# Where the heads stage keeps its substitution matrix and its PSUM banks, and where the last MLP tiles are split: a two-layer attention and RWKV-7 trunk on one core

## The chip, the cores and the metric

One Trainium2 chip, of which the kernel uses one core. The metric is device time in microseconds of one execution. Three executions of the kernel before took 4080.47, 4091.8 and 4091.95 us (median 4091.8).

The core has five engines with a queue each, worked off in order: PE (TensorE, matmul), DVE (VectorE), ACT (ScalarE), POOL (GpSimd) and SP, which here only issues DMAs. SBUF is the working memory of 128 partitions, PSUM the eight banks (128 partitions of 512 f32 each) that PE writes its results to. A "span" is the time from the first to the last instruction of the one execution that was profiled.

## The reference, cut to what matters

Each of two layers normalises and modulates the tokens (1024 latent, 256 context), projects them once, and hands the columns to two groups of heads: eight heads of softmax attention and eight heads of an RWKV-7 recurrence that runs in both directions. Their outputs are joined, projected, and followed by a squared-ReLU MLP. The changed parts are the two groups of heads and the end of the last layer's MLP:

```python
def rwkv7_step(state, inp):                       # group B, per direction and head, over all tokens
    r, w, k, v, a, b = inp
    sa = jnp.einsum('dbhij,dbhj->dbhi', state, a)
    state = state * w[..., None, :] + sa[..., :, None] * b[..., None, :] + v[..., :, None] * k[..., None, :]
    return state, jnp.einsum('dbhij,dbhj->dbhi', state, r)

def attend(q, k, v):                              # group A
    s = jnp.einsum('bqhd,bkhd->bhqk', q, k).astype(jnp.float32) * MLA_SCALE
    p = jax.nn.softmax(s, axis=-1).astype(v.dtype)
    return jnp.einsum('bhqk,bkhd->bqhd', p, v)

def sq_relu_mlp(h, w1, w2):
    return jnp.square(jax.nn.relu(h @ w1)) @ w2

# ... per layer i
x = x + mx[2][:, None] * (jnp.concatenate([att_x, rw_x], axis=-1) @ w_out[i])
x = x + mx[5][:, None] * sq_relu_mlp(modulate(rmsnorm(x, norm2_g[i]), mx[3], mx[4]), w_mlp1[i], w_mlp2[i])
# ... after both layers
return rmsnorm(x, final_g)
```

## The kernel before

A layer runs in three stages: `phase_in` (projections), `heads` (both groups of heads), `phase_out` (output projection and MLP). Products that need full precision split each factor into a high part (an ACT cast to a shorter format) and a low part (the rest, a subtraction on DVE or POOL), and PE makes three matmuls of them.

**The planner.** A stage describes its work as units (`us(engine, ns, ...)`): an engine, an assumed duration, what it needs, what it writes, and for PE units the class of PSUM banks that the result goes to. `Units.run` plays these units through and so sets the order in which each engine's instructions stand; of the units that could start soonest it takes the one with the longest path behind it, shifted by a rank (`RANKS_HEADS` and others, added to the path of the units of that name). The durations, latencies and ranks are numbers in the code. At run time the engines follow that order and wait for each other by semaphores; the assumed durations no longer play a part.

**`heads`.** Two chains share the engines.

- The recurrence (`recurrence`) runs ten steps of 128 tokens in each direction. In a step PE makes the block matrices `A` ("blk", L377; DVE masks them, L381), ACT and DVE lay them out (`begin1`, L414; transpose into `AX`, L419), and then DVE solves 32 small triangular systems per partition by forward substitution: 31 rounds of `mult` (`tmp` = `AX` column times row of `Y`, L436) and `total` (`Y` += `tmp`, L440). `Y`, the matrix of the substitution, lies in SBUF; POOL sets it to unit rows beforehand (L422, L424). ACT copies it out (`end1`, L449), DVE transposes, PE makes products "m1" (L473) and "x2" (L485), and then the state goes through PE products z, u, s, y (L519, L528, L538, L549/L552) for each direction and half step, with ACT and DVE evictions (`S`, L542, L543).
- The attention (`attention`) takes each head and tile of 512 queries: PE tests all scores for their maximum ("max", L715; DVE reduces them, L717, L718), turns the maxima into a row ("rows", L723), makes the scores (L742; ACT takes the exponential into `P`, L747), sums `P` on POOL (`Ps`, L751, 128 columns at a time) and multiplies with the values (L736).

PSUM is divided into classes: three banks "g" for most products, two "x" for the maxima alone, two "z" for the state's products, one "o" for the values' sums. A unit waits for a free bank of its class.

**The last MLP tiles.** In the last layer most of the MLP's second product is made by `fast`; the last 512 hidden columns are left to `finish`, called for the 512-token tile a = 1, and for a = 2 in two parts of 256 tokens. Four tiles of `w2` are loaded into `R`. `finish` splits each of them when a pair of output rows needs it: for a = 1 by ACT (L967) and DVE (L969), for a = 2 once in each part by ACT and POOL (L969), 12 splits in all. It adds the products to `x` (L1558), and then `norm_units` makes the final norm: ACT squares (L877, L880), DVE sums them (`acc`, L881), PE sums over partitions (`qn`, L885), and DVE writes the output (L1570).

Of the kernel before, what the change touches and what calls it, by code (L numbers as in the profile page):

```python
# [99 lines left out]
def sp_ns(n, k=1):  # L100
# [6 lines left out]
RANKS_HEADS = {"mult": -23041, "m1": -18260, "total": 4579, "max": 115, "f3a": -11034, "scores": 327, "sums": 2772, "values": -13437, "y": -22140,  # L107
               "begin1": -12967, "rows": 691, "BKt": -29802, "f1": -1812, "put": -46488, "yp": -1704, "A": -4699, "f1a": -11490, "m1p": -12501,
               "halves": 9522, "end3": -17483, "f2": -881}
# [153 lines left out]
class Trunk:  # L263
# [36 lines left out]
    def heads(self, li, ard, bvd, pc, gated, ysd, kd, vd, qd, qrd, krr, catd):  # L300

        with ExitStack() as es:
            e1 = self.pool(es, "hd", 1)
            ps = self.pool(es, "hps", 1, space=PSUM)
            banks = {k: [ps.tile([128, 512], F32, name=f"ps_{k}{j}") for j in range(n)] for k, n in (("g", 3), ("x", 2), ("z", 2), ("o", 1))}
            tiles = {}


            for name, n, shape in (("YF", 1, [128, 32, 32]), ("AX", 1, [128, 32, 32]), ("XM", 1, [128, 32, 32]), ("Y", 1, [128, 32, 16]), ("tmp", 1, [128, 144]),
# [6 lines left out]
            us = Units(59, RANKS_HEADS, dict(PE=120, ACT=75, DVE=75, Pool=75, SP=2300), False, True, 0.745, 0.395, 100)  # L316
# [6 lines left out]
    def recurrence(self, us, tiles, li, ard, bvd, pc, gated, ysd, catd):  # L323
# [9 lines left out]
        YF, XT, XM, tmp, sq, rs8 = (tiles[k][0] for k in ("YF", "XT", "XM", "tmp", "sq", "rs8"))  # L333
# [3 lines left out]
        half = lambda e: slice(64 * e, 64 * e + 64)  # L337
        heads = [(p, e, half(e)) for p in range(4) for e in range(2)]
# [11 lines left out]
        def step(i):  # L350
            w = {}
# [19 lines left out]
            for d in range(2):  # L371
                for ph in range(2):
                    for e in range(2):
# [9 lines left out]
                        x = add(f"blk{d}", us("PE", 772, back(NA, "begin", "m1", "z0", "z1", "y0", "y1"), pe, 284, bank="g", r=[nar[d], nbv[d]], rows=61))  # L383
                        add("A", us("DVE:A", 707, [x], dve, free=x))


            for d in range(2):
                for ph in range(2):
# [7 lines left out]
                    x = add(f"tok{d}", us("PE", 470, [], pe, 213, bank="g", r=[nbv[d]], rows=121))  # L396
# [10 lines left out]
                x = add(f"tok{d}", us("PE", 480, [], pe, 213, bank="g", r=[nbv[d]], rows=121))  # L407
# [21 lines left out]
            b2 = us("DVE", 1261, w["begin"] + back(NX, "end3"), begin2)  # L429
            b2b = us("Pool", 907, back(NY, "end1"), begin2b)  # L430
# [50 lines left out]
            for d in range(2):  # L481
# [9 lines left out]
                x = add("x2", us("PE", 570, [m1a[d], e3b[0]], pe, bank="g", rows=15))  # L491
# [1236 lines left out]
```

## Time and profile before

| what | before |
|---|---|
| median of three runs | 4091.8 us (4080.47 to 4091.95) |
| the profiled execution | 4084.27 us |
| its span | 4082.5 us |
| PE busy | 3884.9 us (95%) |
| DVE busy | 2595.6 us (64%) |
| ACT busy | 1831.8 us (45%) |
| POOL busy | 1312.9 us (32%) |
| mean granted clock of PE | 0.956 |

On PE the heads stage lasts from 504 to 1166 us in the first layer and from 2615 to 3267 us in the second; `finish` begins at about 4011 us. [...]

### The profile page before, as it was taken

The numbers are of one execution on the slowest core, as the hardware profiler recorded it, in microseconds if no ns is written. First come the engines' busy times: TensorE is split into PE (matmuls) and PEld (weight loads), VectorE is DVE, ScalarE is ACT, GpSimd is POOL, SyncE is SP. The second block draws the span as 40 slices with busy tenths as digits, with TensorE's granted clock in tenths as the row PEclk, the third lists the DMA queues.
The fourth block names the chain that finished last, engine by engine and source line by source line (L and its number), as shares of the span: only waits on it lengthen the run. The fifth ranks groups of instructions, "written<-read, shape, count | busy, mean of one in ns | idle before, by whom it ended". The sixth has DMA issues, their size and how long they took to land.

```text
span 4082.5 us, 66855 instructions
## 1 busy us (share of the span) xinstructions
PE 3884.9 (95%) x26144; PEld 2982.8 (73%) x26144; DVE 2595.6 (64%) x4563; ACT 1831.8 (45%) x3113; POOL 1312.9 (32%) x1912
## 2 busy tenths in 40 slices
PE   6999999999999999999998999999999999999998
PEld 3766666766778888888887766766676678777777
DVE  4477277788747455555337477487877565767676
ACT  4355456676644122222115355556676643333333
POOL 1344254545631000000001244455544704333322
PEclk9999979999999999999999999878998999999999
DMA  6256622332342122222103144711232251111111
GB/s 212 73 171 197 222 81 86 97 91 64 92 159 87 58 78 88 78 73 82 37 32 134 58 160 154 237 47 52 81 103 75 69 201 37 52 47 42 52 55 49
DMA packets 279708, 394.21 MB, mean 97 GB/s; under 512 B 60512, under 2 KB 192576, under 8 KB 279392
## 3 DMA queue, kind: packets, MB, share of 16 engines
q1 hardware_dynamic: 278992, 389.36, 30.0%
q8 instruction: 205, 3.36, 0.3%
q14 instruction: 111, 0.91, 0.1%
q10 hardware_dynamic: 400, 0.59, 0.1%
HBM read 288.45 MB, written 101.42 MB: 95 GB/s over the span
## 4 chain that ended last, share of the span: by engine, by line
PE 71%; DVE 14%; ACT 3%; issue 3%; DMA 2%; POOL 1%; SPq 0%; DVEq 0%; POOLq 0%; ACTq 0%
PE qm L930 39%; PE pm_m L930 8%; PE ps_g L742 4%; DVE tmp L436 3%; PE ps_g L377 3%; DVE Y L440 3%; PE ps_o L736 2%; PE ps_x L715 2%; PE qm L943 1%; DVE nm L717 1%; DMA aw<-in_ada_w 1%; PE pm_n L1185 1%; PE ps_z L549 1%; PE ps_z L552 1%; PE ps_z L538 1%
## 5 line engine op out<-in xcount | busy, mean ns | idle before, releaser
L930 PE MATMUL qm<-hh,wh 128*128 128x512 f32 (+1 forms) x1488 | 556.1, 374 | 7.3 <-DVE x L1529 6.9
L930 PE MATMUL qm<-hh,wl 128*128 128x512 f32 (+1 forms) x1488 | 554.2, 372 | 0.7 <-DVE wl L969 0.7
L930 PE MATMUL qm<-hl,wh 128*128 128x512 f32 (+1 forms) x1488 | 554.3, 373 | 0.0
L751 POOL TENSOR_TENSOR Ps<-Ps,P 128x128 f32<-128x128 f32 x1024 | 442.3, 469 | 256.5 <-ACT P L747 255.5
L967 ACT CAST wh<-wr 128x1024 fp32r<-128x1024 f32 x149 | 155.7, 1045 | 440.8 <-PE qm L930 399.2
L930 PE MATMUL pm_m<-hh,wh 128*128 128x512 f32 (+4 forms) x896 | 339.8, 379 | 3.2 <-ACT o L1244 3.2
L930 PE MATMUL pm_m<-hl,wh 128*128 128x512 f32 (+4 forms) x896 | 330.4, 369 | 1.1 <-POOL hl L917 1.1
L930 PE MATMUL pm_m<-hh,wl 128*128 128x512 f32 (+4 forms) x896 | 331.1, 370 | 0.2 <-DVE wl L969 0.2
L930 PEld LDWEIGHTS qm<-hh,wh 128*128 128x128 f32 x1488 | 279.6, 188 | 65.7 <-DVE x L1529 9.0
L930 PEld LDWEIGHTS qm<-hh,wl 128*128 128x128 f32 x1488 | 279.8, 188 | 55.1 <-DVE wl L969 1.4
L930 PEld LDWEIGHTS qm<-hl,wh 128*128 128x128 f32 x1488 | 279.6, 188 | 55.2 <-DVE hl L1425 0.9
L1529 DVE SCALAR_TENSOR_TENSOR x<-qm,mods,x 128x512 f32<-128x512 f32 x280 | 196.5, 742 | 177.1 <-PE qm L930 176.8
L930 PE MATMUL qm<-uh,wl 128*128 128x512 f32 (+1 forms) x768 | 274.0, 357 | 2.1 <-DVE wl L969 2.1
L930 PE MATMUL qm<-uh,wh 128*128 128x512 f32 (+1 forms) x768 | 275.0, 358 | 0.0
L930 PE MATMUL qm<-ul,wh 128*128 128x512 f32 (+1 forms) x768 | 273.8, 357 | 0.0
L969 DVE TENSOR_TENSOR wl<-wr,wh 128x1024 fp32r<-128x1024 f32 x149 | 188.8, 1267 | 127.9 <-ACT wh L967 127.6
L717 DVE TENSOR_REDUCE nm<-ps_x 128x1 f32<-128x512 f32 (+1 forms) x400 | 222.5, 584 | 68.5 <-PE ps_x L715 66.6
L747 ACT ACTIVATE P<-ps_g 128x512 f32<-128x512 f32 (+1 forms) x336 | 192.2, 587 | 140.2 <-PE ps_g L742 118.8
L1452 DVE SCALAR_TENSOR_TENSOR x<-qm,mods,x 128x512 f32<-128x512 f32 x160 | 119.6, 749 | 196.0 <-PE qm L930 192.6
L436 DVE TENSOR_TENSOR tmp<-AX,Y 128x126 f32<-128x126 f32 (+22 forms) x620 | 224.3, 362 | 21.8 <-ACT AX L427 3.7
L440 DVE TENSOR_TENSOR Y<-Y,tmp 128x126 f32<-128x126 f32 (+22 forms) x620 | 212.7, 343 | 22.4
L930 PEld LDWEIGHTS pm_m<-hh,wh 128*128 128x128 f32 (+2 forms) x896 | 169.8, 190 | 67.1 <-issue 31.0
(348 smaller groups left out, 8786.3 us busy)
## 6 DMA issues: line engine op xcount, KB each, us to landing
wr<-in_w SPq DMA_DIRECT2D x90, 512.0 KB, 3.6
BV<-bv SPq DMA_DIRECT2D x40, 768.0 KB, 4.3
raw<-in_ada_w SPq DMA_DIRECT2D x48, 512.0 KB, 3.9
AR<-ar SPq DMA_DIRECT2D x40, 512.0 KB, 5.9
wr<-in_w_in SPq DMA_DIRECT2D x37, 512.0 KB, 3.8
aw<-in_ada_w SPq DMA_DIRECT2D x32, 512.0 KB, 4.2
bv<-bk SPq DMA_DIRECT2D x32, 512.0 KB, 3.1
ar<-ar SPq DMA_DIRECT2D x32, 512.0 KB, 3.8
```

The source lines that it names most:

```text
L377: nc.tensor.matmul(b[:, 128 * j:128 * j + 128], BK[d][half(e), c, p], AR[d][half(e), 2 * p + c], start=True, stop=True)
L436: nc.vector.tensor_tensor(tm, AX[:, t + 1:32, t:t + 1].to_broadcast(tm.shape), Y[:, t:t + 1, 0:nu].to_broadcast(tm.shape), op=ALU.mult)
L440: nc.vector.tensor_tensor(y, y, tmp[:, 0:ns * nu].rearrange("p (s u) -> p s u", s=ns), op=ALU.add)
L717: us("DVE", 175 + kn * 1.04, [], lambda b, i=i, n=n, kn=kn: nc.vector.tensor_reduce(m3[:, i, n:n + 1], b[:, :kn], AXIS_X, ALU.max), w=[("n ...
L742: nc.tensor.matmul(b[:, :tl], x[:, 128 * n:128 * n + 128], y[:, :tl], start=i == 0, stop=i == 2)
L747: us("ACT", 195 + tl * 0.835, [], lambda b, j=j: nc.scalar.activation(P[j][:, :tl], b[:, :tl], AF.Exp, scale=SCALE), w=[("P", j)], free=x)
L751: us("Pool:sums" if n == 1 else "Pool", 483, [], lambda a=a, b=P[j][:, c:c + 128], c=c: nc.gpsimd.tensor_tensor(sums[:, c:c + 128], a, b, ...
L930: self.nc.tensor.matmul(out, a, b, start=n == 0, stop=n == last)
L967: us("ACT", 947, [], lambda: nc.scalar.copy(wh, raw), r=[key], w=[("wh", j)])
L969: us("Pool" if pool else "DVE:weights", ns, [], lambda: eng.tensor_tensor(wl, raw, wh.bitcast(F32), op=ALU.subtract), r=[key, ("wh", j)], ...
L1452: us("DVE", dve_ns(tl), [u[1]], lambda b: nc.vector.scalar_tensor_tensor(X(m, a), b[:, :tl], self.mods[li][:, 8 * gate + m, s:s + 1], X(m, ...
L1529: z = us("DVE", dve_ns(512), [z], lambda b, m=m, a=a, f=f: nc.vector.scalar_tensor_tensor(X(m, a), b, f, X(m, a), ALU.mult, ALU.add), r=[" ...
```

## The change

1. **`Y` moves to PSUM.** The tile `Y` [128, 32, 16] takes a whole PSUM bank. Since POOL no longer sets it, unit rows are made once per stage in an SBUF tile `Y0`, and ACT copies `Y0` to `Y` before every substitution (`begin2b`).
2. **Six banks, one class.** "g" has six banks; maxima, state products and all else share them. "o" keeps its bank, the eighth holds `Y`.
3. **Durations, latencies and ranks of the heads stage are set anew**, the ranks for each layer apart. This moves instructions on every engine, though no instruction but those of 1 is added or taken away in this stage.
4. **`finish` splits each tile of `w2` once**, into the tiles `hh[0..3]`, `hl[0..3]` that held the MLP's input, and the hidden tile's columns into `hh[4..7]`, `hl[4..7]`. Eight ACT casts and eight POOL subtractions go.

```diff
-RANKS_HEADS = {"mult": -23041, "m1": -18260, "total": 4579, "max": 115, "f3a": -11034, "scores": 327, "sums": 2772, "values": -13437, "y": -22140,
...
+RANKS_HEADS = ({"halves": 6003, "total": -414, "A": 21222, "m1p": -12501, "m1": -28360, "y": -24249, "f2": 3549, "values": -12745, "BKt": -21292,
...
-            banks = {k: [ps.tile([128, 512], F32, name=f"ps_{k}{j}") for j in range(n)] for k, n in (("g", 3), ("x", 2), ("z", 2), ("o", 1))}
-            tiles = {}
+            banks = {k: [ps.tile([128, 512], F32, name=f"ps_{k}{j}") for j in range(n)] for k, n in (("g", 6), ("o", 1))}
+            tiles = {"Y": [ps.tile([128, 32, 16], F32, name=f"ps_Y{li}")]}
...
-            us = Units(59, RANKS_HEADS, dict(PE=120, ACT=75, DVE=75, Pool=75, SP=2300), False, True, 0.745, 0.395, 100)
+            us = Units(59, RANKS_HEADS[li], dict(PE=110, ACT=20, DVE=115, Pool=80, SP=2300), False, True, 0.745, 0.395, 80)
...
+        def unit_rows():
+            nc.gpsimd.memset(Y0, 0.0)
+            for g in range(2):
+                nc.gpsimd.memset(Y0[half(g)].rearrange("p a b -> p (a b)")[:, 16 * g::33], 1.0)
+
+        ones = [us("Pool", 907, [], unit_rows)]
...
             def begin2b():
-                nc.gpsimd.memset(Y, 0.0)
-                for g in range(2):
-                    nc.gpsimd.memset(Y[half(g)].rearrange("p a b -> p (a b)")[:, 16 * g::33], 1.0)
+                nc.scalar.copy(Y, Y0)
...
-            b2b = us("Pool", 907, back(NY, "end1"), begin2b)
+            b2b = us("ACT", 650, back(NY, "end1") + ones, begin2b)
...
-                prev = [us("DVE:mult", 158 + 1.05 * ns * nu, prev, lambda t=t, ns=ns, nu=nu: mult(t, ns, nu), 0, beside=60)]
+                prev = [us("DVE:mult", 73 + 1.05 * ns * nu, prev, lambda t=t, ns=ns, nu=nu: mult(t, ns, nu))]
...
-                    x = add(f"z{d}", us("PE", 567, copies[d] + [az[d]] + w["A"][4 * d:4 * d + 4] + w[f"V{d}"], z_pe, 138, bank="z", rows=121))
+                    x = add(f"z{d}", us("PE", 590, copies[d] + [az[d]] + w["A"][4 * d:4 * d + 4] + w[f"V{d}"], z_pe, 110, bank="g", rows=121))
...
-                           bank="x", r=[("Qh", jq)] + khk, rows=91)
+                           bank="g", r=[("Qh", jq)] + khk, rows=91)
...
             def finish(a, parts):
-                jb = []
+                both = lambda n, k: [(n, k, 1), (n, k, 2)]
...
+                    for n in range(4):
+                        us("ACT", act_ns(1024), [], lambda n=n: nc.scalar.copy(hh[n].t, R[n]), r=[("r", n)], w=both("hh", n))
+                        us("DVE:weights", dve_ns(1024), [], lambda n=n: nc.vector.tensor_tensor(hl[n].t, R[n], hh[n].t.bitcast(F32), op=ALU.subtract), r=[("r", n)] + both("hh", n), w=both("hl", n))
...
-                        if m % 2 == 0:
-                            wh, wl, wk = self.split_weights(us, R[m // 2], ("r", m // 2), tiles, a == 2)
+                        wh, wl, wk = hh[m // 2].t, hl[m // 2].t, both("hh", m // 2) + both("hl", m // 2)
```

How the order moves. First PE at the beginning of the first layer's heads stage, from its seventh row on (`AR`, `BV` are the recurrence's inputs, rows on them are "blk"; `Kh`, `Qh` are high parts of keys and queries, rows on them are "max"; `ps_g`, `ps_x` are banks). Before:

```order
L377 MATMUL ps_g_3472<-AR_3487,BV_3485 128x128 x4
L377 MATMUL ps_g_3471<-AR_3487,BV_3485 128x128 x4
L377 MATMUL ps_g_3472<-AR_3487,BV_3485 128x128 x4
L377 MATMUL ps_g_3471<-AR_3487,BV_3485 128x128 x4
L715 MATMUL ps_x_3473<-Kh_3535,Qh_3528 128x512
L377 MATMUL ps_g_3472<-AR_3488,BV_3486 128x128 x4
L377 MATMUL ps_g_3470<-AR_3488,BV_3486 128x128 x4
L377 MATMUL ps_g_3471<-AR_3488,BV_3486 128x128 x4
L377 MATMUL ps_g_3472<-AR_3488,BV_3486 128x128 x4
L715 MATMUL ps_x_3474<-Kh_3535,Qh_3528 128x512
L715 MATMUL ps_x_3473<-Kh_3535,Qh_3528 128x512
L715 MATMUL ps_x_3474<-Kh_3535,Qh_3528 128x512
```

After, at the same place:

```order
L387 MATMUL ps_g_3470<-AR_3487,BV_3485 128x128 x4
L387 MATMUL ps_g_3471<-AR_3487,BV_3485 128x128 x4
L387 MATMUL ps_g_3472<-AR_3487,BV_3485 128x128 x4
L723 MATMUL ps_g_3475<-Kh_3535,Qh_3528 128x512
L723 MATMUL ps_g_3470<-Kh_3535,Qh_3528 128x512
L723 MATMUL ps_g_3471<-Kh_3535,Qh_3528 128x512
L723 MATMUL ps_g_3472<-Kh_3535,Qh_3528 128x512
L723 MATMUL ps_g_3475<-Kh_3535,Qh_3528 128x512
L723 MATMUL ps_g_3473<-Kh_3535,Qh_3528 128x512
L723 MATMUL ps_g_3470<-Kh_3535,Qh_3528 128x512
L723 MATMUL ps_g_3474<-Kh_3535,Qh_3528 128x512
L723 MATMUL ps_g_3471<-Kh_3535,Qh_3528 128x256
```

The maxima of the first tile, which stood one to three at a time between other products, now stand twelve in a row (the last three of them follow the rows shown), in banks that the other products use too. On DVE the first transposition into `AX` (L419 before) stood behind 5 of the 584 ns reductions; it now stands behind 26. Over the whole stage no run of maxima was longer than three before; of the 208 in the first layer's stage, 90 now stand in 13 runs of five to twelve, and in the second layer's 11 such runs hold 71 of 192.

Then POOL at the end of the program (`t` are sums of hidden columns for `fast`; `r` the loaded weights; `wh`, `wl` the high and low parts; `rs` the norm's factors). Before:

```order
L1518 TENSOR_TENSOR t_4_26540<-u_3_26555 128x512
L969 TENSOR_TENSOR wl_0_26535<-r_0_26566,wh_0_26534 128x1024
L969 TENSOR_TENSOR wl_2_26517<-r_1_26567,wh_2_26516 128x1024
L969 TENSOR_TENSOR wl_2_26519<-r_2_26568,wh_2_26518 128x1024
L889 TENSOR_TENSOR rs_0_26543<-rs_0_26543,mh 128x4
L969 TENSOR_TENSOR wl_0_26535<-r_3_26569,wh_0_26534 128x1024
L969 TENSOR_TENSOR wl_2_26517<-r_0_26566,wh_2_26516 128x1024
L969 TENSOR_TENSOR wl_2_26519<-r_1_26567,wh_2_26518 128x1024
L969 TENSOR_TENSOR wl_0_26535<-r_2_26568,wh_0_26534 128x1024
L889 TENSOR_TENSOR rs_0_26543<-rs_0_26543,mh 128x2
L969 TENSOR_TENSOR wl_2_26517<-r_3_26569,wh_2_26516 128x1024
L889 TENSOR_TENSOR rs_0_26543<-rs_0_26543,mh 128x2
```

After:

```order
L1525 TENSOR_TENSOR t_2_26504<-u_3_26521,u_1_26519 128x512
L1516 TENSOR_TENSOR r_0_26532<-r_0_26532,r_1_26533 128x1024
L1525 TENSOR_TENSOR t_3_26505<-u_2_26520 128x512
L1516 TENSOR_TENSOR r_1_26533<-r_1_26533,r_3_26535 128x1024
L1525 TENSOR_TENSOR t_4_26506<-u_3_26521 128x512
L897 TENSOR_TENSOR rs_0_26509<-rs_0_26509,mh 128x4
L897 TENSOR_TENSOR rs_0_26509<-rs_0_26509,mh 128x2 x2
```

All eight subtractions are gone from POOL. On PE, five products of `fast` now stand between the last hidden product and the first product of `finish` (one before), and the norm's first sum over partitions (`qn`) stands behind the first two products of the second tile (before: directly behind the last product of the first tile).

## Rows read from the trace of the kernel before

**Rows 1.** Stretches: us; busy PE, PEld, DVE, ACT, POOL; PE's clock; DMA.

```profile
504.00:560.00 56.00, 52.14 (x207) 40.56 (x207) 35.73 (x79) 23.62 (x31) 28.47 (x35) 0.57 0.44 143
560.00:1160.00 600.00, 570.50 (x6654) 408.62 (x6655) 462.61 (x1066) 409.75 (x741) 339.01 (x680) 0.95 0.27 80
...
2615.00:2690.00 75.00, 64.17 (x267) 47.54 (x266) 44.85 (x108) 33.63 (x44) 41.91 (x59) 0.68 0.51 166
2690.00:3262.00 572.00, 537.04 (x6164) 383.44 (x6164) 430.88 (x983) 383.09 (x682) 307.89 (x622) 0.91 0.24 72
...
4010.90:4071.40 60.50, 52.31 (x313) 46.52 (x312) 47.61 (x72) 25.89 (x42) 20.88 (x10) 0.94 0.13 48
```

**Rows 2.** PE's waits, first heads stage: waiting <- waited for: total us, times, longest.

```profile
PE ps_g L723 <- DVE nm L718: 8.5, 3, 4.2
PE ps_x L715 <- DVE nm L717: 6.2, 11, 1.2
...
PE ps_z L549 <- DVE S L542: 2.4, 2, 2.3
```

**Rows 3.** The same for the second heads stage.

```profile
PE ps_g L723 <- DVE nm L718: 8.4, 2, 5.3
PE ps_x L715 <- DVE nm L717: 6.7, 7, 2.1
PE ps_z L549 <- DVE S L542: 6.5, 2, 6.1
```

**Rows 4.** PE in order of time (start, us, line), and its stretch behind that wait.

```profile
886.72 0.74 PE L723 MATMUL ps_g<-identr,nm 128*128 128x128 f32 x4 [4.16 <-DVE nm L718]
...
887.00:898.00 11.00, 11.00 (x134) 7.93 (x132) 8.30 (x30) 7.35 (x17) 2.21 (x5) 0.69 0.06 17
```

**Rows 5.** DVE in order of time, same place.

```profile
879.73 5.78 DVE L436 TENSOR_TENSOR tmp<-AX,Y 128x31 f32<-128x31 f32 x1 [0.81 <-POOL Ps L751]
```

**Rows 6.** POOL in order of time, same place.

```profile
874.24 10.00 POOL L751 TENSOR_TENSOR Ps<-Ps,P 128x128 f32<-128x128 f32 x24 [8.70 <-ACT P L747]
```

**Rows 7.** The substitution's products: count, ns min/median/max, first and last start.

```profile
L436 DVE TENSOR_TENSOR tmp<-AX,Y x620: 162/285/7207, 534.2 to 3212.4; 128x126 f32<-128x126 f32 x15, 128x30 f32<-128x30 f32 x10, 128x78 f32<-128x78 f32 x10, 128x110 f32<-128x110 f32 x10
```

**Rows 8.** The page's groups: busy us, mean ns, idle before.

```profile
L717 DVE TENSOR_REDUCE nm<-ps_x 128x1 f32<-128x512 f32 (+1 forms) x400 | 222.5, 584 | 68.5 <-PE ps_x L715 66.6
...
L436 DVE TENSOR_TENSOR tmp<-AX,Y 128x126 f32<-128x126 f32 (+22 forms) x620 | 224.3, 362 | 21.8 <-ACT AX L427 3.7
L440 DVE TENSOR_TENSOR Y<-Y,tmp 128x126 f32<-128x126 f32 (+22 forms) x620 | 212.7, 343 | 22.4
```

**Rows 9.** DVE in order of time: a substitution round with POOL idle.

```profile
594.07 0.26 DVE L440 TENSOR_TENSOR Y<-Y,tmp 128x96 f32<-128x96 f32 x1
```

**Rows 10.** Instructions on `S`: one source in PSUM, and both in SBUF.

```profile
L542 DVE TENSOR_TENSOR S<-ps_z,S x76: 385/416/425, 596.4 to 3243.3; 128x256 f32<-128x256 f32 x76
L543 DVE TENSOR_TENSOR S<-S,pc x76: 424/426/2872, 596.8 to 3243.8; 128x256 f32<-128x256 f32 x76
```

**Rows 11.** Instructions on `Y` of ACT and POOL.

```profile
L449 ACT COPY YF<-Y x40: 640/657/672, 573.2 to 3214.0; 64x512 f32<-64x512 f32 x40
L422 POOL MEMSET Y<- x20: 524/529/537, 505.2 to 3152.2; 128x512 f32 x20
```

**Rows 12.** PE in order of time: matmuls of 512 columns at full clock.

```profile
1114.03 0.39 PE L742 MATMUL ps_g<-Qh,Kl 97*128 97x512 f32 x1
1114.26 0.40 PE L742 MATMUL ps_g<-Ql,Kh 97*128 97x512 f32 x1
```

**Rows 13.** `finish`: PE's wait for the norm, and POOL's splits by line.

```profile
PE qn L885 <- DVE acc L881: 7.5, 2, 4.3
...
L969 POOL TENSOR_TENSOR wl<-r,wh 128x1024 fp32r<-128x1024 f32 x8 | 19.2, 2405 | 101.9 <-ACT wh L967 101.9
```

**Rows 14.** `finish` in order of time, DVE and POOL.

```profile
4026.38 2.46 DVE L881 TENSOR_TENSOR acc<-acc,t 128x512 f32<-128x512 f32 x1 [0.92 <-ACT t L880]
...
4025.90 2.40 POOL L969 TENSOR_TENSOR wl<-r,wh 128x1024 fp32r<-128x1024 f32 x1 [86.20 <-ACT wh L967]
```

More of the change, by code (lines that the diff above doesn't have):

```diff
@@ L381, in dve @@
                             nc.vector.tensor_tensor(A[:, it + e:it + 8:2], b.rearrange("p (n a t) -> p n a t", n=4, a=2), mask.rearrange("p (a t) -> p a t", a=2).unsqueeze(1).to_broadcast([128, 4, 2, 64]), op=ALU.mult)
-                        x = add(f"blk{d}", us("PE", 772, back(NA, "begin", "m1", "z0", "z1", "y0", "y1"), pe, 284, bank="g", r=[nar[d], nbv[d]], rows=61))
-                        add("A", us("DVE:A", 707, [x], dve, free=x))
+                        x = add(f"blk{d}", us("PE", 900, back(NA, "begin", "m1", "z0", "z1", "y0", "y1"), pe, 120, bank="g", r=[nar[d], nbv[d]], rows=61))
+                        add("A", us("DVE:A", 598, [x], dve, free=x))
             for d in range(2):
@@ L414, in begin1 @@
                     nc.scalar.copy(YF[q].rearrange("p t n -> p n t"), A[64 + 32 * h:96 + 32 * h, :, 0, q])
-                add("begin", us("ACT:begin1", 1970, w["A"] + back(1, "begin2"), begin1))
+                add("begin", us("ACT:begin1", 1990, w["A"] + back(1, "begin2"), begin1))
             def begin2():
@@ L461, in step @@
             e1s = [add("end1", us("ACT", 681, prev + back(1, "end2"), lambda g=g: end1(g))) for g in range(2)]
-            e2 = add("end2", us("DVE", 1994, e1s + back(1, "m1", "x2"), end2))
-            e2b = add("end2", us("DVE", 1266, e1s, end2b))
-            e3b = [add("end3", us("ACT:end3", 1970, [e2b] + back(2, "u0", "u1") + zero, lambda j=j: end3b(j))) for j in (1, 0)]
+            e2 = add("end2", us("DVE", 2000, e1s + back(1, "m1", "x2"), end2, 35))
+            e2b = add("end2", us("DVE", 1250, e1s, end2b, 35))
+            e3b = [add("end3", us("ACT:end3", 2000, [e2b] + back(2, "u0", "u1") + zero, lambda j=j: end3b(j))) for j in (1, 0)]
             m1a, X = [], []
@@ L580, in step @@
                     if need:
-                        x = add(f"y{d}", us("PE:yp", 1226, [uev] + sdep, y_pe, bank="z", r=[nar[d]], rows=100))
-                        ev = add(f"yev{d}", us("ACT:y" if first else "DVE", 397 if first else 444, [x] + (back(2, "spill", "fin") if first else again), y_ev, free=x))
+                        x = add(f"y{d}", us("PE:yp", 1226, [uev] + sdep, y_pe, bank="g", r=[nar[d]], rows=100))
+                        ev = add(f"yev{d}", us("ACT:y" if first else "DVE", 397 if first else 334, [x] + (back(2, "spill", "fin") if first else again), y_ev, free=x))
             if need and first:
@@ L764, in total @@
                     nc.tensor.matmul(b[:, i:i + 1], Ps[js][:, 128 * i:128 * i + 128], c1, start=True, stop=True)
-            x = us("PE", 45 + 208 * nq, [], total, 180, bank="g", r=[("Ps", js, 128 * i) for i in range(nq)], rows=1)
-            us("DVE", 199, [], lambda b: nc.vector.reciprocal(rc[:, :nq], b[:, :nq]), w=["rc"], free=x)
+            x = us("PE", 845 / 4 * nq, [], total, 145, bank="g", r=[("Ps", js, 128 * i) for i in range(nq)], rows=1)
+            us("DVE", 92, [], lambda b: nc.vector.reciprocal(rc[:, :nq], b[:, :nq]), w=["rc"], free=x)
             us("Pool", 206 + 54 * nq, [], lambda: nc.gpsimd.tensor_copy(rx[:, :nq], rc[:, :nq].unsqueeze(2).to_broadcast([128, nq, 64])), r=["rc"], w=["rx"])
```

72 lines of the change are left out of this document (38 added, 34 removed).

## The prediction

> **What bounds the kernel now.** I read the stretches of both heads stages and of `finish` first [rows 1]; the rest of the program keeps its instructions and nearly its order. The columns to look at are PE's busy time and its granted clock. In the middle of the heads stages PE is busy for 570.5 of 600 us and for 537.0 of 572, at 0.95 and 0.91 of full speed. So PE is the bound, with two leaks: 29.5 + 35.0 = 64 us in which it stands, and 5% of 600 + 9% of 572 = 30 + 51 = 81 us that the lower clock level takes. The beginnings of the stages (504 to 560, 2615 to 2690) lose 4 + 11 us standing and 24 + 24 us to the clock. DVE is busy for 463 of 600 and 431 of 572 us, ACT for 68%, POOL for some 55%: none of them is a bound on average, but each can keep PE waiting for a moment.
>
> Second, whom PE waits for in these stages [rows 2, 3]: almost always DVE. The three groups shown of each stage make 17.1 + 21.6 = 39 us; maxima (L718, L717) lead, the state `S` follows.
>
> Third, one such wait from close by [rows 4 to 6]. At 879.73 us DVE begins a substitution product of 31 elements, which should take some 0.2 us; it takes 5.78. POOL adds `Ps` without a pause from 874.24 on for 10.00 us, followed by another instruction with no gap. The product has both sources in SBUF, and it comes to an end only when POOL does. Behind it in DVE's queue stand the last maxima; PE waits 4.16 us for them, and in the 11 us after that its clock is 0.69, which takes another 0.31 × 11 = 3.4 us. A wait of PE thus costs about 1.8 times its length here. The longest substitution product takes 7.2 us, the median 0.285 [rows 7].
>
> How much that is in all: the two substitution lines take 224.3 + 212.7 = 437 us for 1240 instructions [rows 8]. A round has 92 elements on average (31 rounds of (31-t)(t/2+1), 2856 together), and a round with 96 takes 0.26 us when POOL is idle [rows 9]. 1240 × 0.26 = 322, so 115 us of DVE's time, 57 a stage, is waiting for POOL.
>
> **Part 1: `Y` in PSUM.** Both substitution instructions then have one source in SBUF and one in PSUM. The nearest rows are the two on `S`, of equal shape [rows 10]: with one source in PSUM the longest of 76 takes 425 ns, with both in SBUF the longest takes 2872. The first kind never waited for POOL. I therefore take the 115 us as gone. A PSUM source costs nothing in itself there (median 416 against 426 ns). No row shows DVE writing to PSUM, which `total` will do 620 times. Ends: nothing, or, if the second memory were charged once more like a whole short instruction (162 ns, the shortest product [rows 7]), 620 × 0.16 = 100 us; below nothing is excluded, as the same elements are written. I take nothing, since reading costs nothing.
>
> [...]
>
> What 115 us less on DVE are worth on the path: only what PE waits for. Of the 39 us I let three quarters go, 29 us (the rest waits for true work of DVE, or for `S` products with both sources in SBUF, which stay). With 0.8 us of clock per us of wait, as in the example, 29 × 1.8 = **52 us**. Both ends: none of it, and all 39 × 1.8 = 70.
>
> ACT gets 20 copies `Y0` to `Y`. The nearest row is the copy of `Y` out, 657 ns [rows 11]: 20 × 0.66 = 13 us, on an engine busy for 68%. Each needs only that the previous `Y` has been copied out; behind it in ACT's queue stand exponentials for `P` and evictions. Ends 0 and 13; I take 1, as the copy stands in front of a longer layout copy that the substitution needs as well. POOL loses 20 fillings of 0.53 us and the small ones after them: it is off the path, nothing.
>
> **Parts 2 and 3: banks, durations, ranks.** No PE instruction is added, so nothing changes but who waits. Gain: the 6.2 + 6.7 us that maxima wait for one of two banks are in the 39 already. Cost: maxima now come in runs. PE makes one of 512 columns in 0.23 us (start to start [rows 12]), DVE reduces one in 0.58 [rows 8]. There are 24 runs of five and more, 161 maxima, 6.7 a run; after a run DVE is 6.7 × 0.35 = 2.3 us behind, with all six banks full or nearly. What PE has next in a shared bank waits, up to 2.3 × 1.8 = 4.2 us a run. The new order sets attention products or the values' bank behind most runs and other DVE work far off; I charge two runs, **8 us**; ends 0 and 24 × 4.2 = 101. At the beginning 21 more reductions stand ahead of the first transposition: 21 × 0.58 = 12 us, of which DVE had 20 idle of 56 us, so it covers most; the recurrence starts up to 12 us later, and its DVE chain becomes shorter by 57 us over ten steps, which pays for that. I charge nothing. The clock lost at the beginnings (48 us) I leave as it is, with no row for the new mixture.
>
> Sum for the heads: 52 - 1 - 8 = **43 us**.
>
> **Part 4: `finish`.** POOL's eight subtractions (19.2 us, 2.4 each [rows 13]) and eight ACT casts go. The norm's sums on DVE have both sources in SBUF, and they too wait for POOL: the one at 4026.38 takes 2.46 us and ends just after POOL's instruction, which ran from 4025.90 for 2.40 [rows 14]. That lies on the path: PE waits 7.5 us for these sums [rows 13]; in 4010.9 to 4071.4 it stands for 8.2 us and loses 6% of 60.5 = 3.6 us to the clock, 11.8 in all [rows 1]. With the norm's sum also two products further back, nearly all of that should go: **10 us**, ends 6 and 12. The added wait: the new splits overwrite the MLP's input, so they wait for the last hidden product. ACT then needs one relu and one cast (1.6 us), DVE a subtraction (1.2), and PE has five products of `fast` meanwhile, 30 matmuls × 0.23 = 7 us. Covered; without that cover it would be 3 us. The 11 us behind the last product (last norm, output) stay.
>
> **Sum.** 43 + 10 = 53 us off the profiled execution: 4084.3 - 53 = 4031. That execution is 7.5 us under the median of the runs shown and 4 over the fastest; two of three runs stand at 4092, so I put the median of the changed kernel at the same value, rounded to **4030 us**.
>
> **The rivals.**
>
> *The whole of DVE's waits goes.* DVE's durations become steady, so the planner's order meets what it was made for, and the beginnings also gain half of their lost clock: 70 + 24 + 10 = 104, time 3980. For it: the largest single waits all sit on stalls like the one shown. Against it: on a PE that is busy for 95%, something else is late next. With two thirds of all that PE loses in these stages (64 + 81 + 15 + 48 = 208) it would be 3935. Chance 0.22.
>
> *Only the tail counts.* PE is the bound, and the waits that go are replaced by others of the new order: 4084 - 10 = 4074. For it: an order of a thousand products a stage has never run, and 39 us are 3% of the stages. Against it: the stalls were random to the planner, and they go. Chance 0.15.
>
> *PSUM costs what SBUF saved.* With the upper end of part 1, 100 of the 115 us are eaten, and 0.13 × 52 = 7 remain: 4084 - 7 + 9 - 10 = 4076. For it: no row shows `total`'s write. Against it stand the `S` rows. Chance 0.06. [...]
>
> *Maxima hold the shared banks (slower).* All six banks full of unreduced maxima while z, u, s or y of the recurrence is next on PE. Price 4.2 us a run; above (52 - 1 + 10)/4.2 = 15 of the 24 runs the kernel is slower than before; with all, 4084 - 61 + 101 = 4124. For it: before, such a product had its own class and could not be held by a maximum. Against it: DVE is 57 us less busy per stage, and what follows a run was chosen with reductions known. Chance 0.09.
>
> **How the numbers follow.** Forecast 0.48, and the four rivals 0.22, 0.15, 0.06, 0.09. About 0.3% (12 us) is what a measurement of this kernel can tell from no change, so "faster" means under 4079. Faster: 0.48 + 0.22, six tenths of "only the tail" (0.09) and of the PSUM case (0.04), together 0.83. Within 0.3%: 0.09. Slower: 0.08. The range leaves out the slower case above and the deepest part of the first rival below: 3950 to 4080.
>
> **What would show each step.** Right: no substitution instruction over 0.6 us, the two lines together near 320 us instead of 437; PE's waits for L718/L717 and `S` under a third of [rows 2, 3]; a clock of 0.96 or more in the middle of both stages; no POOL split after 4000 us and a wait for `acc` under 2 us. Wrong: products of `total` longer than 0.30 us at 96 elements (PSUM is charged), or long waits of recurrence products for reductions (banks), or a middle of the stages whose PE idle and clock stay at 30 and 0.95: then DVE's stalls were cover for something else.

## The result, and the profile after

The changed kernel takes 3978.57 us (median of four runs, 3969.47 to 3987.16) where the kernel before takes 4089.7: a ratio of 0.9731, 95% interval 0.9711 to 0.9751, or 111 us less. The forecast was 4030, with a range of 3950 to 4080. The profiled execution of the changed kernel took 3976.51 us, with a span of 3974.7.

The heads stage lasts from 504.2 to 1123.4 us in the first layer and from 2583.0 to 3174.1 us in the second: 619.2 instead of 661.3 us, and 591.1 instead of 644.1. From its second end to the end of the program it is 800.6 us instead of 814.8. What lies between the two stages is nearly as long as before (1459.6 and 1457.6). So 95 us come from the heads and 14 from `finish`.

The stretches after, cut like [rows 1] at the new places (us; busy PE, PEld, DVE, ACT, POOL; PE's clock; DMA):

```profile
504.00:560.00 56.00, 50.79 (x273) 37.72 (x274) 40.75 (x97) 33.00 (x44) 38.59 (x59) 0.83 0.48 142
560.00:1118.00 558.00, 545.14 (x6590) 390.42 (x6588) 393.08 (x1049) 401.89 (x740) 317.65 (x626) 0.96 0.29 85
2583.00:2650.00 67.00, 63.55 (x312) 47.72 (x314) 50.90 (x127) 35.75 (x48) 42.16 (x68) 0.76 0.49 151
2650.00:3168.00 518.00, 501.54 (x6104) 361.66 (x6102) 369.88 (x964) 380.96 (x685) 283.31 (x570) 0.95 0.27 79
3900.00:3963.00 63.00, 62.35 (x373) 55.30 (x371) 47.19 (x85) 20.03 (x37) 1.72 (x2) 1.00 0.11 40
```

Against [rows 1], PE in the middle of the stages stands for 12.9 + 16.5 = 29 us instead of 64, and the clock is 0.96 and 0.95 instead of 0.95 and 0.91: most of what the clock gives back in the middles lies in the second stage. In the beginnings the clock is 0.83 and 0.76 instead of 0.57 and 0.68. (The clock is that of TensorE as a share of full speed; in the execution before it stands at 0.50 from 535 to 545 us and at 1.00 from 1200 to 1210.) `finish` has the full clock and 0.65 us without work on PE.

The substitution, the copy of unit rows and the state's scaling (count, ns min/median/max):

```profile
L444 DVE TENSOR_TENSOR tmp<-AX,ps_Y x620: 157/254/297, 539.2 to 3099.3; 128x126 f32<-128x126 f32 x15, 128x30 f32<-128x30 f32 x10, 128x78 f32<-128x78 f32 x10, 128x110 f32<-128x110 f32 x10
L448 DVE TENSOR_TENSOR ps_Y<-ps_Y,tmp x620: 172/269/307, 539.4 to 3099.5; 128x126 f32<-128x126 f32 x15, 128x30 f32<-128x30 f32 x10, 128x78 f32<-128x78 f32 x10, 128x110 f32<-128x110 f32 x10
...
L432 ACT COPY ps_Y<-Y x20: 589/590/597, 505.8 to 3056.0; 128x512 f32<-128x512 f32 x20
...
L551 DVE TENSOR_TENSOR S<-S,pc x76: 424/426/5599, 588.0 to 3142.3; 128x256 f32<-128x256 f32 x76
```

Where the longest product took 7207 ns [rows 7], no substitution instruction takes more than 307. The scaling of `S`, whose sources both stayed in SBUF, still has one of 5599, and its 76 instructions together take 52.0 us, where they took 43.0 before. The groups of the whole run (busy us, mean ns, idle before), beside [rows 8]:

```profile
L725 DVE TENSOR_REDUCE nm<-ps_g 128x1 f32<-128x512 f32 (+1 forms) x400 | 213.4, 583 | 38.1 <-PE ps_g L723 36.9 <-ACT G L540 0.2
...
L448 DVE TENSOR_TENSOR ps_Y<-ps_Y,tmp 128x126 f32<-128x126 f32 (+22 forms) x620 | 161.5, 261 | 18.5
L444 DVE TENSOR_TENSOR tmp<-AX,ps_Y 128x126 f32<-128x126 f32 (+22 forms) x620 | 154.6, 249 | 39.0 <-ACT AX L435 22.2
```

The two substitution lines take 316 us instead of 437. Last, PE's waits in the first heads stage (the whole list down to 1 us) and, behind the dots, those of the second; the same view as [rows 2, 3]:

```profile
PE ps_g L401 <- DMA BV<-bv: 5.7, 2, 5.5
PE ps_g L723 <- ACT Qh L716: 3.7, 3, 2.2
PE ps_g L527 <- ACT G L585: 3.4, 1, 3.4
PE ps_g L780 <- POOL rx L776: 2.9, 2, 1.7
PE ps_g L387 <- issue: 2.6, 1, 2.6
PE ps_g L481 <- DVE XM L460: 1.6, 1, 1.6
PE ps_o L744 <- DVE ob L768: 1.1, 4, 0.4
PE ps_g L723 <- DVE nm L725: 1.0, 4, 0.3
...
PE ps_g L401 <- DMA BV<-bv: 6.0, 1, 6.0
PE ps_g L527 <- ACT G L585: 4.2, 3, 2.0
...
PE ps_g L723 <- DVE S L550: 1.9, 1, 1.9
...
PE ps_g L750 <- DVE nm L725: 1.4, 1, 1.4
```

DVE is no longer at the head of either list. What leads is one load at the start of each stage (`BV`), which was there before too.

### The profile page after: what moved, and what is told of

The parts are those of the page before. It is cut to its first block, busy times and chain, and to the rows that moved or that the text cites. A ratio compares the mean times of both kernels' runs of the same rounds, so it can differ in the third digit from the quotient of the medians.

```text
span 3974.7 us, 66881 instructions
## 1 busy us (share of the span) xinstructions
PE 3819.7 (96%) x26144; PEld 2939.4 (74%) x26144; DVE 2463.1 (62%) x4563; ACT 1826.9 (46%) x3125; POOL 1267.8 (32%) x1850
## 4 chain that ended last, share of the span: by engine, by line
PE 76%; DVE 9%; DMA 3%; issue 2%; ACT 2%; POOL 1%; SPq 0%; DVEq 0%; POOLq 0%; ACTq 0%
PE qm L938 41%; PE pm_m L938 8%; PE ps_g L750 5%; PE ps_o L744 3%; PE ps_g L723 2%; PE ps_g L387 2%; PE qm L951 1%; PE ps_g L536 1%; PE ps_g L527 1%; PE ps_g L546 1%; PE ps_g L481 1%; PE ps_g L401 1%; PE ps_g L557 1%; PE ps_g L560 1%; PE pm_n L1192 1%
## 5 line engine op out<-in xcount | busy, mean ns | idle before, releaser
L759 POOL TENSOR_TENSOR Ps<-Ps,P 128x128 f32<-128x128 f32 x1024 | 433.8, 462 | 308.2 <-ACT P L755 307.9
L725 DVE TENSOR_REDUCE nm<-ps_g 128x1 f32<-128x512 f32 (+1 forms) x400 | 213.4, 583 | 38.1 <-PE ps_g L723 36.9
L938 PEld LDWEIGHTS pm_m<-hl,wh 128*128 128x128 f32 (+2 forms) x896 | 169.3, 189 | 33.6 <-POOL hl L925 2.2
L938 PEld LDWEIGHTS pm_m<-hh,wl 128*128 128x128 f32 (+2 forms) x896 | 169.6, 189 | 30.7 <-issue 0.7
```

The lines of the kernel that those rows point to most:

```text
L725: us("DVE", 63 + kn * 1.048, [], lambda b, i=i, n=n, kn=kn: nc.vector.tensor_reduce(m3[:, i, n:n + 1], b[:, :kn], AXIS_X, ALU.max), w=[("n ...
L759: us("Pool:sums" if n == 1 else "Pool", 415, [], lambda a=a, b=P[j][:, c:c + 128], c=c: nc.gpsimd.tensor_tensor(sums[:, c:c + 128], a, b, ...
L938: self.nc.tensor.matmul(out, a, b, start=n == 0, stop=n == last)
```

## Experiments

The theory: DVE's instructions with two sources in SBUF wait for POOL's bursts of sums, and this alone cost PE its pauses and its clock. The rivals: the six shared banks bring the gain, or the new durations and ranks do, or `finish`. The first group takes the change apart. The kernels of a group ran on one chip beside the kernel before.

### `finish` alone

The kernel before, with only part 4 of the change.

> The kernel before with the new `finish` alone; the heads stage is untouched. The end of the program became 14 us shorter in the changed kernel (814.8 to 800.6 us from the end of the second heads stage). Both theories: 10 to 14 us under the kernel before, ratio 0.9966 to 0.9976, and PE waits under 3 us for `acc`. If the heads stage's change also helped the end, less than 5 us.

Measured: 4076.64 us against 4089.42, ratio 0.9962 (0.9944 to 0.9979). From the end of the second heads stage to the end of the program it is 800.3 us (814.8 before), and PE waits 2.9 us for `acc`, as in the changed kernel. The stretch of `finish`:

```profile
4009.00:4070.00 61.00, 59.96 (x363) 53.37 (x361) 45.47 (x82) 18.12 (x34) 1.72 (x2) 1.00 0.12 44
```

So part 4 is worth 13 to 16 us by itself, and the heads bring the rest.

### Six banks in one class, numbers of before, `Y` in SBUF and then in PSUM

Two kernels with the new `finish`, six banks "g" and the copy of unit rows by ACT, but with before's durations and ranks. They differ in one line:

```diff
-            tiles = {"Y": [e1.tile([128, 32, 16], F32, name=f"Y{li}")]}
+            tiles = {"Y": [ps.tile([128, 32, 16], F32, name=f"ps_Y{li}")]}
```

> The new `finish`, six banks in one class, and the copy of unit rows by ACT, but `Y` in SBUF and the durations and ranks of before. Theory (the substitution's waits for GpSimd are what cost the time): nothing gained over the `finish` alone beyond 8 us, so 4065 to 4085; the two substitution lines stay near 437 us together. Rival (the shared banks bring the gain): 4020 or less.

> As the kernel with six banks and the old numbers, but `Y` in PSUM: the one difference is where `Y` lies. Theory (waits for GpSimd): the substitution takes 316 us instead of 437 and the time falls by at least 40 us against the same kernel with `Y` in SBUF, to 4020 or less. Rival (the new numbers and the order they make bring the gain): the substitution falls as much, but the time by less than 15 us, to 4055 or more.

Measured: 4065.82 us with `Y` in SBUF (ratio 0.9937, 0.9914 to 0.9961) and 3988.89 in PSUM (0.9749, 0.9723 to 0.9774). The substitution takes 436 us in the first and 317 in the second. The banks without PSUM can't be told from `finish` alone; the place of `Y` is worth 77 us, and in both traces DVE, ACT and POOL run the same instructions in the same order (PE's starts differ in 4 of 26144 places). Both heads stages of the first kernel:

```profile
502.70:1190.20 687.50, 632.62 (x6876) 454.12 (x6876) 501.16 (x1149) 440.52 (x784) 363.59 (x689) 0.88 0.28 83
2649.20:3265.30 616.10, 583.88 (x6432) 417.12 (x6432) 469.21 (x1093) 419.96 (x733) 337.85 (x643) 0.90 0.29 85
```

and of the second:

```profile
502.90:1137.40 634.50, 614.54 (x6876) 443.89 (x6876) 437.05 (x1149) 438.89 (x784) 358.30 (x689) 0.91 0.30 90
2595.00:3185.30 590.30, 568.14 (x6432) 408.38 (x6432) 425.91 (x1093) 418.56 (x733) 331.23 (x644) 0.93 0.30 89
```

DVE is busy for 107 us less (970.4 to 863.0). PE has the same instructions; it stands for 42 us instead of 87, and is busy for 34 us less at the higher clock. That makes 79 us for 45 us of standing, 1.75 us of time for each. PE's largest waits in the first stage of the kernel with `Y` in SBUF show how DVE's delay reaches PE:

```profile
PE ps_g L524 <- ACT G L582: 9.8, 6, 2.9
PE ps_g L478 <- DVE nm L722: 7.3, 1, 7.3
PE ps_g L720 <- ACT Qh L713: 5.9, 1, 5.9
PE ps_g L408 <- DVE nm L722: 5.5, 1, 5.5
```

Two of them name ACT. L582 copies the state that DVE's scaling has made; with `Y` in PSUM it is not among the waits of 1 us and more in this stage.

### The changed kernel with `Y` back in SBUF

The same line the other way round. Each engine's instructions stand in the order of the changed kernel; only two neighbouring DMAs on SP change places.

> The changed kernel with `Y` back in SBUF; every engine's instructions stand in the same order as in the changed kernel, one bank lies idle. Theory (waits for GpSimd): DVE waits again for some 115 us, PE's waits for maxima come back and the clock falls below 0.96; 4030 to 4070. Rival (numbers and order): 3980 to 3995, with DVE's waits beside the path. A third reading, that both are needed: 4000 to 4030.

Measured: 4138.98 us, ratio 1.0121 (1.0096 to 1.0146). That is 160 us over the changed kernel (by the ratios as well) and 50 over the kernel before, more than any theory had expected. The stages, and PE's first wait in the first of them:

```profile
504.20:1206.30 702.10, 645.70 (x6876) 459.55 (x6876) 503.90 (x1150) 436.42 (x784) 366.32 (x689) 0.87 0.27 81
2663.00:3329.70 666.70, 612.50 (x6432) 436.30 (x6432) 484.19 (x1093) 419.59 (x734) 337.13 (x643) 0.85 0.26 79
```

```profile
PE ps_g L723 <- DVE nm L725: 28.4, 10, 9.2
```

The substitution is back at 462 us. PE stands for 56 + 54 = 111 us instead of 43, and waits 28.4 us for maxima in runs that cost it 1.0 in the changed kernel. These are waits of the maxima themselves for a bank that is not yet reduced. In the second stage no group leads like this; the 54 us are spread over many. So the new order, with its long runs of maxima, is better only where DVE does not stall. By before's numbers the place of `Y` is worth 77 us, by the new ones 160.

### Shorter sums on POOL

To see whether POOL is what `Y` in SBUF waits for, POOL's later sums were cut to 4 columns, once with `Y` in SBUF and once, as a control, in PSUM:

```diff
-                    a = (P[jp[0]] if n == 1 else sums)[:, c:c + 128]
+                    a, w = (P[jp[0]] if n == 1 else sums)[:, c:c + 128], 128 if n == 1 else 4
...
+ b=(P[j][:, c:c + w] if n > 1 else self.ident)
```

> The changed kernel with `Y` in SBUF, and POOL's later sums `Ps` made on 4 columns instead of 128 (1024 of its 1168 additions; the first of each tile adds the identity matrix, so the attention's denominators are not computed: that part is left out). Every engine's instructions stand in the same order as with `Y` in SBUF and full sums (4138.98 us). Theory (POOL's bursts of sums hold up DVE's instructions with two SBUF sources): the substitution falls from 462 us to under 350 and the time to 4020 or less. Rival (`Y` in SBUF costs the time by itself, whatever POOL does): substitution over 430 us and 4110 or more.

> The control: the changed kernel (`Y` in PSUM) with the same short sums, the denominators left out likewise. It shows what shorter sums are worth where DVE doesn't wait for them. Theory: within 15 us of the changed kernel's 3978.6, and within 20 us of the kernel with `Y` in SBUF and short sums. Rival: 3950 or less, if POOL's sums were late for PE by themselves; then only the difference to the kernel with `Y` in SBUF counts.

Measured: 4054.79 us (ratio 0.9925, 0.9898 to 0.9951) in SBUF and 3959.88 (0.9703, 0.968 to 0.9727) in PSUM. With `Y` in SBUF, the substitution and POOL's sums:

```profile
L444 DVE TENSOR_TENSOR tmp<-AX,Y 128x126 f32<-128x126 f32 (+22 forms) x620 | 192.8, 311 | 42.1 <-ACT AX L435 25.3
L448 DVE TENSOR_TENSOR Y<-Y,tmp 128x126 f32<-128x126 f32 (+22 forms) x620 | 190.1, 307 | 18.4
...
L759 POOL TENSOR_TENSOR Ps<-Ps,P 128x4 f32<-128x4 f32 x1024 | 174.1, 209 | 553.2 <-ACT P L755 551.4
...
L759 POOL TENSOR_TENSOR Ps<-P,ct 128x128 f32<-128x128 f32 x144 | 63.9, 472 | 65.2 <-ACT P L755 65.2
...
L717 POOL TENSOR_TENSOR Ql<-Qraw,Qh 96x512 fp32r<-96x512 f32 (+1 forms) x40 | 46.8, 1171 | 29.0 <-ACT Qh L716 25.2 <-PE ps_g L772 3.5
L700 POOL TENSOR_TENSOR Kl<-Kraw,Kh 64x1280 fp32r<-64x1280 f32 x16 | 46.7, 2920 | 24.6 <-ACT Kh L699 24.4
```

and POOL's sums with `Y` in SBUF and full sums:

```profile
L759 POOL TENSOR_TENSOR Ps<-Ps,P 128x128 f32<-128x128 f32 x1024 | 444.7, 470 | 386.2 <-ACT P L755 385.8
...
L759 POOL TENSOR_TENSOR Ps<-P,P 128x128 f32<-128x128 f32 x144 | 63.6, 470 | 117.0 <-ACT P L755 116.8
```

All bounds of the theory were missed: 350 us, 4020 us, and the 20 us between the two kernels, which came out at 95; the control is 19 us under the changed kernel (11 by the ratios), where 15 were expected. The rivals' bounds were missed as well. An addition of 4 columns still takes 0.21 us, so POOL's sums fell only to 174 + 64 us, from 445 + 64. The substitution fell from 462 to 383 us: with 316 as what it takes without waits, 67 of 146 us of waiting are left. That 46% are left where 47% of POOL's time on sums is left looks like a proportion, but it is chance: sums are not all that DVE waits for. One product of the kernel with short sums and the POOL instructions beside it, in order of time:

```profile
839.09 3.82 DVE L444 TENSOR_TENSOR tmp<-AX,Y 128x108 f32<-128x108 f32 x1
...
839.03 2.93 POOL L700 TENSOR_TENSOR Kl<-Kraw,Kh 64x1280 fp32r<-64x1280 f32 x1 [0.44 <-ACT Kh L699]
841.91 1.76 POOL L759 TENSOR_TENSOR Ps<-P,ct 128x128 f32<-128x128 f32 x4
```

`Kl` and `Ql` are the low parts of keys and queries, which POOL makes by a subtraction. Most of these 3.82 us is one `Kl`. I gave the waiting of each of the 1240 substitution instructions (its time above the median of its shape with `Y` in PSUM) to the POOL instruction that it overlaps longest. With full sums 82 of the 146 us lie beside sums, 49 beside `Kl` and `Ql` and 13 beside the products with the gate (L637, L640); with short sums 15, 38 and 12 of the 67. So what was cut are the waits for sums, and most of what is left belongs to POOL's other instructions. And SBUF has no share by itself: the instructions that overlap none of POOL's, 627 with full and 759 with short sums, take at most 303 ns, and together they are no longer than the same shapes with `Y` in PSUM. In the kernel before it is the same: 693 such instructions, at most 301 ns, and all of the waiting in the other 547, about half of it beside sums and a third beside `Kl` and `Ql`. So the theory was right that DVE waits for POOL, and wrong that it waits for the sums alone. In time, the price of SBUF fell from 160 to 95 us.

### Old bank classes with `Y` in PSUM

`Y` takes one bank of eight. Two kernels keep before's separate classes and numbers and give up one bank, of the state's class or of the class of most products:

```diff
-(("g", 6), ("o", 1))
+(("g", 3), ("x", 2), ("z", 1), ("o", 1))
...
+(("g", 2), ("x", 2), ("z", 2), ("o", 1))
```

> Y in PSUM, new `finish`, the durations, ranks and bank classes of before with one state bank less (3, 2, 1, 1), since `Y` takes one. It shows whether PSUM alone is enough. Theory (DVE's waits are most of it): 3985 to 4025, within 30 us of the same with six banks in one class (3988.9). Rival (the shared class is needed to pay for `Y`'s bank): 4040 or more, with PE waiting for the one state bank.

> As the kernel with `Y` in PSUM and the old classes at 3, 2, 1, 1 banks (4154.5 us), but the bank is taken from the class of most products: 2, 2, 2, 1. It tells apart why that kernel was slower. If the single state bank was the reason: 4030 or less. If any six banks that are divided are too few for these products: 4090 or more, with clock and idle time of PE as bad as there (0.85 to 0.87 in the heads stages, 73 us).

Measured: 4154.45 us (ratio 1.0193, 1.0164 to 1.0221) and 4155.04 (1.0166, 1.0123 to 1.0208), 165 us over the same kernel with one class (3988.89), 170 to 180 by the ratios. My theory for the first was wrong; it gave the bank almost no price. The stages of the first of the two:

```profile
503.90:1221.10 717.20, 677.18 (x6876) 478.80 (x6876) 450.73 (x1149) 438.91 (x784) 356.59 (x687) 0.85 0.27 79
2682.20:3337.90 655.70, 622.52 (x6432) 436.51 (x6432) 430.93 (x1093) 420.43 (x733) 331.95 (x642) 0.87 0.27 80
```

The substitution is as fast as in the changed kernel (316 us), so its stalls are not the reason. PE stands for 73 us instead of 42, and is busy for 117 us more at a clock of 0.85 and 0.87: most of the loss is clock. The second kernel has 72 us and 0.88 and 0.85. So it does not matter which of these two classes gives up the bank (the maxima's was not tried). A planner with fewer free banks also makes another order, and what is the bank's price and what the order's stays open.

### The state's sum in PSUM as well

One wait of the old kind is left in the heads stages, the scaling of `S` (5599 ns at most). Its first step can leave the sum in the bank that it reads, with no instruction more:

```diff
-nc.vector.tensor_tensor(S1, v3(b[:, 0:256], a=4), S0, op=ALU.add)
-nc.vector.tensor_tensor(S1, S1, pc[:, d, :, 2 * i + c].unsqueeze(2).to_broadcast([128, 4, 64]), op=ALU.mult)
+nc.vector.tensor_tensor(v3(b[:, 0:256], a=4), v3(b[:, 0:256], a=4), S0, op=ALU.add)
+nc.vector.tensor_tensor(S1, v3(b[:, 0:256], a=4), pc[:, d, :, 2 * i + c].unsqueeze(2).to_broadcast([128, 4, 64]), op=ALU.mult)
```

> The changed kernel with the sum of the new state kept in its PSUM bank, so that the scaling of `S` reads PSUM and SBUF instead of two SBUF sources; order and number of instructions unchanged. In the changed kernel that scaling takes 52.0 us for 76, of which 76 x 0.426 = 32.4 without waits; ACT waits 40.6 us for its results. Theory: no scaling over 0.45 us, 20 us less on DVE, and 5 to 20 us less time: 3958 to 3974. Rival (these waits are covered by other products): 3974 to 3983.

Measured: 3950.45 us, ratio 0.9687 (0.9661 to 0.9713). That is under the 3958 to 3974 expected; on this chip the kernel before took 4081.84 us, and by the ratios the gain over the changed kernel is 18 us, inside the 5 to 20. Both steps:

```profile
L551 DVE TENSOR_TENSOR S<-ps_g,pc x76: 423/424/426, 599.0 to 3108.1; 128x256 f32<-128x256 f32 x76
```

```profile
L550 DVE TENSOR_TENSOR ps_g<-ps_g,S x76: 418/429/433, 598.6 to 3107.6; 128x256 f32<-128x256 f32 x76
```

No scaling is longer than 426 ns. In that execution the heads stages lasted 609.0 and 564.7 us, with a clock of 0.95 in both. A second group put the changed kernel, this one and the same step with before's numbers on one chip:

> The changed kernel itself, beside the two others of this group: 3970 to 3987, ratio to the kernel before 0.971 to 0.975.

> The changed kernel with the state's sum in PSUM once more, now on one chip with the changed kernel itself: 12 to 24 us under it (ratio to it 0.994 to 0.997). Rival (the first comparison caught a difference of chips): within 6 us.

> `Y` in PSUM, six banks and the new `finish` with the durations and ranks of before (3988.9 us), and the new state's sum kept in PSUM. Theory (each DVE instruction with two SBUF sources in these chains costs by itself): 12 to 25 us less than without the state's sum in PSUM, so 3964 to 3977, as the changed kernel gained 18 by it. Rival (only the new order leaves these waits open): within 6 us of 3989.

Measured: the changed kernel 3975.23 us (0.972, 0.9692 to 0.9748), with the state's sum in PSUM 3956.14 (0.9683, 0.9657 to 0.9708), with before's numbers and that sum in PSUM 3977.28 (0.9733, 0.9709 to 0.9758). The gain over the changed kernel is 19 us on one chip (expected: 12 to 24); it is the fastest kernel of this study. With before's numbers the step is worth 12 us by the medians and 6.5 by the ratios (0.9749 to 0.9733), too little to tell.

## Why the prediction was right, and where its sizes were off

Direction and mechanism held; the time came out 51 us under the forecast, on the first rival's 3980. Term by term:

- **The 115 us of waiting, and nothing for PSUM.** Right. The lines fell from 437 to 316 us (322 were predicted). `total`, for which no row stood, takes 250 to 266 ns at 96 elements in 40 instructions, beside 260 before [rows 9]. The waiting was for POOL, as the overlaps under "Shorter sums on POOL" show, but not only for `Ps`: a third of it lies beside `Kl` and `Ql`.
- **What that is worth on the path: 52 predicted.** Too small by some 10 to 15 us. In the middles of the stages standing fell by 35 us (64 to 29) and the clock's loss by 27 to 33 (81 to 48 from the two digits shown, 79 to 51 from three), so 62 to 68 together; the rival's 39 × 1.8 = 70 was nearly that. The waits were set too low: I counted three groups in each stage, 39 us, and let a quarter of them stay, 10 us; 5 are left (3.3 for maxima, 1.9 for `S`). With the smaller groups, which I had not counted, the waits that name DVE fell from 49 to 9 us. And some of DVE's delay reaches PE under ACT's name. The longest such wait before, in order of time:

```profile
2905.43 0.40 ACT L577 COPY G<-S 64x256 f32<-64x256 f32 x1 [5.72 <-DVE S L543]
...
2906.49 1.11 PE L391 MATMUL ps_g<-ct,BV 128*128 128x128 f32 x4 [4.77 <-ACT BKt L394]
```

  PE waits for ACT's copy `BKt`, which stands in ACT's queue behind a copy of the state that waited for DVE. The factor 1.8, read from one example, came out well where only `Y`'s place differs (1.75), but it is no constant: over both stages as wholes PE stood 36 us less (661.3 - 625.3 and 644.1 - 601.0 before, 619.2 - 598.5 and 591.1 - 568.6 after) and was busy for 59 us less, 2.6 us of time for each us of standing.
- **"The clock lost at the beginnings I leave as it is."** This is the step that was furthest off: a term put at nothing that measured some 22 us. By the same reckoning (length times what the clock lacks) the loss fell from 24 + 23 to 9 + 16 us. Standing did not change. The 11 us that the prediction read for the second beginning hold 6 us ahead of the stage's first matmul; from there on:

```profile
2623.60:2690.00 66.40, 61.37 (x255) 45.63 (x255) 44.85 (x108) 31.67 (x40) 33.55 (x46) 0.66 0.46 149
```

  so 4 + 5 us stood against 5 + 3 after. The gain goes with the shared class, whatever the numbers and the place of `Y`: from 504 to 560 us the ten profiled executions with one class have a clock of 0.70 to 0.91, the four with divided classes 0.57 to 0.69. Two executions of one and the same kernel stand at 0.70 and 0.91, so this stretch varies much by itself, and the order differs between the classes too; why the clock is higher stays open. The 60 us after that have 0.94 before; with one class and `Y` in SBUF they have 0.74 and 0.72 (with short sums 0.97), in PSUM 0.89 and 0.98. So with one class the gain is lost again there when DVE waits for POOL's full sums. The rival had 24 us here, but from DVE's steadiness, and the clock is as high in the beginnings of the kernels where DVE is not steady: its number was luck.
- **Maxima hold shared banks: 8 charged.** PE waits 1.4 + 1.9 us for reductions of maxima in the two stages, so the charge was too high. The slower rival came near to a true mechanism: with `Y` in SBUF the same order is slower than before. But there it is the maxima that wait for banks, 28.4 us in one stage; the recurrence's products z, u, s and y, which the rival named, wait 3.4 us for reductions in both. That DVE must not fall behind was its condition, and the change sees to that.
- **`finish`: 10.** 14 on the trace, 13 to 16 in the runs of it alone. PE's wait for `acc` is 2.9 us, where under 2 was expected, and no POOL split is left. The clock of that stretch went to 1.00.
- **The copies by ACT.** 20 × 0.59 = 12 us of ACT, where 13 were estimated; nobody waits for them in the lists shown.
- **What would show each step.** All signs came as named, but two: the clock in the middle of the second stage is 0.95, not 0.96, and the wait for `acc`.
- **What the prediction did not see.** It took banks and numbers for a small cost. With divided classes the kernel with `Y` in PSUM is 165 us slower than with one class, more than `Y`'s place in PSUM gains, so parts 1 and 2 pay only together. The new numbers bring 10 us once `Y` is in PSUM, inside the intervals, and lose 73 without it (4138.98 against 4065.82). So of the 111 us, 13 to 16 are `finish` and 77 the place of `Y` (at before's numbers and with one class); the other 20 or so, banks and numbers, no single comparison tells from nothing.

So of the 55 us by which the profiled execution came out lower than forecast, some 22 are the beginnings, 10 to 15 the middles, 9 the charges for maxima and copies (8 and 1), which these net figures leave no room for, and 4 `finish`; the rest, some 5 to 10, this reckoning does not place. The first rival was the better forecast. PE's waits in the heads stages name DVE for 49 us before and 9 after, ACT for 22 and 18, DMAs for 16 and 17, POOL for 3 and 6; so on a PE busy for 95%, no other engine's waits took the place of DVE's.

## What to carry to other kernels

Where the longest of an instruction is twenty times its median, look at what the other engines do at that moment; if DVE's sources both lie in SBUF and POOL is at work, in a burst or in one long instruction, try moving one of them to PSUM. Here that ended the stall (the longest product fell from 7207 to 297 ns, the longest scaling of `S` from 5599 to 426) and had next to no price on the instruction (429 instead of 416 ns for the state's sum, 250 to 266 instead of 260 for `total` at 96 elements). Count such a stall not only where PE names the stalled engine but in all of PE's standing time, and expect the clock to add to it: here a us of standing cost 1.75 us of time by `Y`'s place alone, and 2.6 in the change as a whole. And look where the bank for it comes from: with before's numbers the same edit gave 0.975 of the time before with the other six banks in one class, and 1.017 or 1.019 with them divided.

## What the runs showed of the hardware

- DVE's wait lasts longer than one instruction of POOL: 5.78 us in [rows 5]. From 879.73 to 884.24 us POOL made the last of its additions, of 10.00/24 = 0.42 us each [rows 6], so about 11, and then a subtraction, with whose end (885.45) the product ends too (885.51):

```profile
884.17 1.28 POOL L709 TENSOR_TENSOR Ql<-Qraw,Qh 96x512 fp32r<-96x512 f32 x1
```

  So some 12 of POOL's instructions in a row ran, without a gap, within that one DVE instruction, which had two SBUF sources. With one source in PSUM no such length shows: the scaling of `S` takes 5599 ns at most with two SBUF sources and 426 with one, the substitution's instructions 7207 and 307.
- DVE reading and writing the same PSUM bank in place is hardly slower than the same into SBUF: 429 ns for the state's sum into PSUM (median of 76), 416 into SBUF before [rows 10]; for `total` 250 to 266 ns at 96 elements, 260 before [rows 9].
- The granted clock took more of the time than PE's pauses themselves: over both stages PE was busy for 1226 us before, 1167 after and 1145 with the state's sum in PSUM, for the same 13308 matmuls, at a clock of 0.92 and 0.88, 0.94 and 0.92, and 0.95 in both, and stood for 79, 43 and 28 us. But the sum of the pauses does not say what the clock will be: with divided classes PE stood for 73 and 72 us, less than before, and was busy for 1300 and 1312, at 0.85 and 0.87 and at 0.88 and 0.85. What kept the clock lower there, no run here shows.
